# MLP of the second block: the first block of the up projection as eight products of quarters, its weights loaded before the mixer's last matmuls, sums of x made beside it

## The chip, the cores and the metric

One core of a Trainium2 chip runs the whole program. The metric is the device time of one execution in microseconds (us). The engines are named as in the profile: PE (TensorE matmuls), PEld (its weight loads), DVE (VectorE), ACT (ScalarE), POOL (GpSimd), SP (SyncE, whose queue issues the DMAs).

## The reference, cut to what matters

The model is two blocks: two layers of attention, mLSTM and SSD with a mixture of experts, then one hybrid layer (gated delta rule and RG-LRU) with an MLP, over 512 tokens of width 1024 in float32. The change concerns the MLP at the end of the second block alone (`d_ff` is 4096, taken in 8 blocks of 512 columns by the kernel):

```python
x = x + jnp.einsum("bse,ed->bsd", mix, w_out.astype(dt))
m = rmsnorm(x, norm_mlp_w)
u = jax.nn.relu(jnp.einsum("bsd,df->bsf", m, w_ff1.astype(dt)))
x = x + jnp.einsum("bsf,fd->bsd", u * u, w_ff2.astype(dt))
...
return rmsnorm(x, final_norm_w)
```

## The kernel before, in words

**Split numbers.** Every float32 operand of a large matmul is kept as two float32r tiles, a high and a low part (`HL`). `split` (L128 to L139) makes them: a cast on ACT writes the high part (L134), a subtraction on DVE or POOL writes the low part (L139). `mm` (L122 to L126) then issues three matmuls: high by high, low by high, high by low.

**The MLP's products.** For each of the 8 blocks of 512 columns, `up(b)` computes relu(m @ w1)^2 with seven products instead of eight. The weights of a block are four quarters (two halves of the 1024 input rows by two halves of 256 columns), x is four quarters too (two halves of the input rows by two halves of 256 tokens): B11, B21, B12, B22. The seven products take sums of weight quarters and sums of x quarters (T1 to T4), and sums of the products are the four quarters of the result. One product is 24 matmuls of 128x256 (two halves of columns, four row tiles, three split matmuls each). `up_part(b, n, u)` makes the weights of product n: with n = 0 it loads two raw tiles of 1 MB (L254), with n = 2 it makes three sums on DVE (L260, L261, L262), with n = 5 a fourth (L264), and it splits the operand, the low part on POOL for n of 1 and 6 and on DVE otherwise. `down(b)` multiplies by w2: 96 matmuls of 128x512 into four PSUM banks `dn`, each emptied on DVE by an addition to R (L1837). The order is up(0), up(1), down(0), up(2), down(1), and so on to down(7).

**The mixer before it, and the joint.** The MLP's input is R plus the second half of the mixer's output projection (`out_last`, additions to R at L1866), which runs by token tiles i = 0 to 3 of 128 tokens. After each tile `fin(i)` takes the rms norm (sum of squares on ACT, L1326; the root on DVE, L158 to L166; the scaling on DVE, L1333, which reads the gain from the tile `sw`) and `mlp_in` transposes the result (PE, L1770) into PSUM banks `tr`, copies it to the float32 tiles X32 (ACT, L1771) and makes the x operands. In the profile X32 is named uTh and uTl, whose space it takes. For tiles 0 and 1 these are B11 and B21; for tiles 2 and 3 `mlp_in` also makes the four sums of x (L1779, L1780, L1783, L1786) and splits T1 to T4 and B22. Two weight operands of block 0 (`w0`, named T3 and T4, whose space they take) are made before the mixer's last matmuls, and `fin(2)` issues the first two products of block 0 with them (named dn<-B11,T3 and dn<-B21,T4 in the profile). The other five operands of block 0 are tasks in the plan, made when their ring slots are free.

**What sets the order.** Weight tiles stand in a list (`plan`); `pump` takes the next one when its ring of split tiles has a free slot, and the raw tiles come from two pools of two buffers each (raw0 and, after the mixer, raw1). Instructions of the functions here are put in order on each engine's queue by the framework's scheduler, so the order of the queues differs from that of the code. Sums of weights use the tile `sw` (`q[4]` at n = 2), which also holds the norm's gain until the last L1333 has read it.

Of the kernel before, what the change touches and what calls it, by code (L numbers as in the profile page):

```python
# [26 lines left out]
UNIT = 1024  # L27
# [43 lines left out]
class Kernel:  # L71
# [169 lines left out]
    def by_k(u):  # L241
        u = u.rearrange("p (k n) -> p k n", k=4)
        return [u[:, k] for k in range(4)]

    def up_part(self, b, n, u):

        v = self.nc.vector
        if n == 0:
            self.quarters = []
            for j in range(2):  # L250
                raw = self.t(self.raws[self.nraw % len(self.raws)].pool, "raw", [P, 2 * UNIT])
                self.nraw += 1
                at = b * 512 + j * 256
                self.nc.sync.dma_start(raw.rearrange("p (k n) -> p k n", n=256),  # L254
                                       self.a["w_ff1_2"][0][:, at:at + 256].rearrange("(k p) n -> p k n", p=P))
                self.quarters += [raw[:, 0:UNIT], raw[:, UNIT:2 * UNIT]]
        q = self.quarters
        if n == 2:
            q.append(self.t(self.mlpp, "sw", [P, UNIT]))
            v.tensor_tensor(q[4], q[2], q[3], op=OP.add)  # L260
            v.tensor_tensor(q[2], q[0], q[2], op=OP.subtract)  # L261
            v.tensor_tensor(q[0], q[4], q[0], op=OP.subtract)  # L262
        if n == 5:
            v.tensor_tensor(q[1], q[1], q[0], op=OP.subtract)  # L264
        self.split(u, q[(0, 1, 0, 4, 2, 1, 3)[n]], "act", "pool" if n in (1, 6) else "dve")
# [1490 lines left out]
        x.close()  # L1756
        return mix[0]

    def mlp_in(self, m, i, n, X, X32):


        nc, v = self.nc, self.nc.vector
        tk, half = slice(i % 2 * P, i % 2 * P + P), i // 2
        cut = lambda n: HL(X[n].h[:, :, tk], X[n].l[:, :, tk])
        ps = []
        for g in range(2):
            p = self.ps("tr", [P, 4, P])
            for j in range(4):
                f = 4 * g + j
                nc.tensor.transpose(p[:, j, :], n[:, f * P:(f + 1) * P], self.ident)  # L1770
            nc.scalar.copy(X32[g][:, :, i * P:(i + 1) * P], p)  # L1771
            if not half:
                self.split(cut(("B11", "B21")[g]), p)
            ps.append(p)
        if not half:
            return
        (b11, b12), (b21, b22) = [[x[:, :, z + i % 2 * P:z + i % 2 * P + P] for z in (0, 256)] for x in X32]
        t2 = self.t(m, "u2", [P, S], bufs=2).rearrange("p (k t) -> p k t", k=4)
        v.tensor_tensor(b11, b12, b11, op=OP.subtract)  # L1779
        v.tensor_tensor(t2, b22, b11, op=OP.subtract)  # L1780
        self.split(cut("T2"), t2)
        self.split(cut("T1"), b11)
        v.tensor_tensor(b12, b22, b12, op=OP.subtract)  # L1783
        self.split(cut("T3"), b12)
        self.split(cut("B22"), ps[1])
        v.tensor_tensor(b21, b21, t2, op=OP.subtract)  # L1786
        self.split(cut("T4"), b21)

    def up_product(self, p, w, x):
        for z in range(2):  # L1790
            for k in range(4):
                self.mm(p[:, z * 256:(z + 1) * 256], w[k][:, z * P:(z + 1) * P], x[:, k, :], start=k == 0, stop=k == 3)

    def mlp(self, m, X, R, begun, finish):

        nc, v = self.nc, self.nc.vector
        uT = {}

        def up(b):
            u_ = self.hl(m, "uT", [P, 4, S], bufs=2)  # L1800
            s1, s5, s3, _ = [t[:, z:z + S] for t in [self.t(m, "nrm", [P, D], bufs=2) for _ in range(2)] for z in (0, S)]

            def keep(f, t, x, y):

                u = self.t(m, "u2", [P, S], bufs=2)
                v.tensor_tensor(u, x, y, op=OP.add)  # L1806
                v.scalar_tensor_tensor(u, u, 0.0, u, op0=OP.max, op1=OP.mult)  # L1807
                d = HL(*(x[:, 2 * f:2 * f + 2, 256 * t:256 * t + 256] for x in (u_.h, u_.l)))
                self.split(d, u.rearrange("p (f t) -> p f t", f=2), "act")

            def product(n, x):
                p = self.ps(("mm", "tr")[n % 2], [P, S])
                self.up_product(p, self.take(("up", b, n)), X[x])
                self.done(("up", b, n))
                return p

            A, C = (product(0, "B11"), product(1, "B21")) if b else begun
            nc.scalar.copy(s1, A)
# [21 lines left out]
            for hf in range(2):  # L1840
                self.done(("dn", b, hf))

        up(0)
        for b in range(8):
            if b < 7:
                up(b + 1)
            if b == 6:
# [3 lines left out]
                finish = lambda i: fin(i, g2)  # L1851
            down(b)

    def second(self):
        nc, a, v = self.nc, self.a, self.nc.vector
        with ExitStack() as c:
            rp = self.pool(c, "res2")
            R = self.t(rp, "R", [P, NT, D])
# [11 lines left out]
            rp = self.pool(c, "mlp")  # L1870
            self.mlpp = rp
            g = self.t(rp, "sw", [P, D])
            self.bcast_load(g, a["norm_mlp_w_2"][0], D)
            X, begun = {}, []

            w0 = [self.hl(rp, t, [P, UNIT]) for t in ("T3", "T4")]
            for n in range(2):
                self.up_part(0, n, w0[n])
            for t in ("B11", "B21", "B22", "T1", "T2"):
                X[t] = self.hl(rp, t, [P, 4, 256])  # L1880
            X32 = self.hl(rp, "uT", [P, 4, S], bufs=2)
            X32 = [x.bitcast(F32) for x in (X32.h, X32.l)]

            def fin(i):
                n = self.t(rp, "nrm", [P, D], bufs=2)
                if i == 2:
                    for z in range(2):
                        p = self.ps("dn", [P, S])
                        self.up_product(p, self.by_k(w0[z]), X[("B11", "B21")[z]])
                        begun.append(p)  # L1890
                    for t in ("T3", "T4"):
                        X[t] = self.hl(rp, t, [P, 4, 256])
                self.rms(rp, n, R[:, i], g, jk=n)
                self.mlp_in(rp, i, n, X, X32)
                self.dump("x3", R[:, i], i)

            self.out_last(mixT, [("out2", q) for q in (2, 3)], add, [4, 5, 6, 7, 0, 1, 2, 3], fin)
# [1 line left out]
            with ExitStack() as x1:  # L1899
# [8 lines left out]
                        nc.sync.dma_start(self.out[0, i * P:(i + 1) * P, :], o)  # L1908
                    self.dump("out", o, i)

                self.mlp(rp, X, R, begun, finish)

    def plan(self):

        a, T = self.a, []
        add = lambda *z, **k: T.append(Task(*z, **k))
        for l in range(2):
            w = a["w_in"][l]
# [24 lines left out]
        w = a["w_in_2"][0]  # L1943
# [10 lines left out]
        w2 = a["w_ff2_2"][0]  # L1954

        def up(b):
            for n in range(0 if b else 2, 7):
                add(("up", b, n), "p", [], 4, 256)
                T[-1].make = lambda u, n=n: self.up_part(b, n, u)

# [282 lines left out]
```

## Time and profile before

| what | value |
|---|---|
| median of 3 runs | 1737.26 us (1736.63 to 1739.16) |
| the profiled execution's own time | 1732.17 us |
| its span, first to last instruction | 1730.3 us |
| mean granted clock of TensorE | 0.954 |
| PE busy in the span | 1561.6 us (90%) |
| DVE busy | 1298.5 us (75%) |
| ACT busy | 827.2 us (48%) |
| POOL busy | 561.3 us (32%) |

The own time is 1.87 us over the span: what lies before the first and after the last instruction. The shares are averages over stages with different limits. The MLP begins at about 1360 us of the span and ends with it. A table of windows tells for stretches of the span how busy each engine was and which clock TensorE was granted; the waits tell what ended an engine's idle time; the timeline gives single instructions with their start and duration. A matmul's duration includes the time in the array's pipeline: its rate is read from the distance between starts.

### The profile page before, as it was taken

Reading aid. Unit: us, or ns where it says so; the run is one execution under the profiler, and the core shown is the slowest. Engines: PE = TensorE matmul, PEld = TensorE weight load, DVE = VectorE, ACT = ScalarE, POOL = GpSimd, SP = SyncE. Lnnn points to the kernel's source line nnn. Section 1 sums busy time; section 2 is a strip of 40 time slices with the busy share of each in tenths; the row PEclk is TensorE's granted clock in tenths of the full one; section 3 lists DMA queues with packets and bytes.
Section 4 is the critical chain, followed back from the end, with each engine's and each line's share of the span. In section 5 each row is a group of like instructions: output and inputs, shape, how many; then the busy total and the mean of one; then the engine's idle time right before and its main releaser. Section 6 shows DMA issues by size and latency. Waiting matters only on the chain. (4 is left out here: it accounts for less than half of the span.)

```text
span 1730.3 us, 29609 instructions
## 1 busy us (share of the span) xinstructions
PE 1561.6 (90%) x11539; PEld 1398.0 (81%) x11539; DVE 1298.5 (75%) x2480; ACT 827.2 (48%) x1422; POOL 561.3 (32%) x464
## 2 busy tenths in 40 slices
PE   7899999699956899997889993999799799999997
PEld 6789899698946789887878972887578698899996
DVE  6847963789957847865689977777776797777774
ACT  4354562278856344551368863555532533333331
POOL 0555332316114555334315202003411143444341
PEclk9999999899987999999989996999999899999999
DMA  5214123499945211123399964432112243333311
GB/s 183 61 59 147 64 103 115 180 363 357 396 166 204 61 59 48 50 86 131 127 346 358 373 239 170 128 98 74 38 52 75 73 127 117 98 98 98 98 62 49
DMA packets 107662, 248.02 MB, mean 143 GB/s; under 512 B 9460, under 2 KB 70776, under 8 KB 95224
## 3 DMA queue, kind: packets, MB, share of 16 engines
q1 hardware_dynamic: 101624, 225.05, 37.4%
q0 software_dynamic: 5888, 20.97, 3.8%
q8 instruction: 94, 1.54, 0.4%
q14 instruction: 56, 0.46, 0.1%
HBM read 218.21 MB, written 27.79 MB: 142 GB/s over the span
## 5 line engine op out<-in xcount | busy, mean ns | idle before, releaser
L134 ACT CAST wh<-raw 128x1024 fp32r<-128x1024 f32 (+3 forms) x375 | 377.5, 1024 | 278.4 <-PE mm L126 70.3
L139 POOL TENSOR_TENSOR wl<-raw,wh 128x1024 fp32r<-128x1024 f32 (+3 forms) x117 | 281.3, 2414 | 474.7 <-ACT wh L134 469.0
L139 DVE TENSOR_TENSOR wl<-raw,wh 128x1024 fp32r<-128x1024 f32 (+2 forms) x258 | 307.2, 1211 | 64.3 <-ACT wh L134 63.4
L124 PE MATMUL mm<-wh,actTh 128*128 128x256 f32 (+2 forms) x640 | 189.5, 297 | 22.2 <-ACT wh L134 7.9
L126 PE MATMUL mm<-wh,actTl 128*128 128x256 f32 (+2 forms) x640 | 185.7, 292 | 2.9 <-POOL actTl L139 2.4
L125 PE MATMUL mm<-wl,actTh 128*128 128x256 f32 (+2 forms) x640 | 185.9, 291 | 0.5 <-DVE wl L139 0.5
L124 PE MATMUL mm<-actTh,wh 128*128 128x512 f32 x368 | 150.5, 409 | 2.4 <-DVE FD L509 0.8
L126 PE MATMUL mm<-actTh,wl 128*128 128x512 f32 x368 | 148.0, 402 | 0.0
L125 PE MATMUL mm<-actTl,wh 128*128 128x512 f32 x368 | 148.0, 402 | 0.0
L124 PEld LDWEIGHTS mm<-wh,actTh 128*128 128x128 f32 x640 | 124.9, 195 | 25.2 <-ACT wh L134 7.9
L126 PEld LDWEIGHTS mm<-wh,actTl 128*128 128x128 f32 x640 | 123.9, 194 | 5.4 <-POOL actTl L139 3.3
L125 PEld LDWEIGHTS mm<-wl,actTh 128*128 128x128 f32 x640 | 124.8, 195 | 1.8 <-DVE wl L139 0.9
L1089 POOL DMA_INDIRECT G<-Xd,idx x32 | 77.9, 2434 | 131.1 <-DVE oh L1138 58.3
L124 PE MATMUL dn<-wh,uTh 128*128 128x512 f32 x256 | 100.9, 395 | 3.1 <-DVE R L1837 3.1
L126 PE MATMUL dn<-wh,uTl 128*128 128x512 f32 x256 | 100.4, 392 | 0.0
L125 PE MATMUL dn<-wl,uTh 128*128 128x512 f32 x256 | 100.1, 391 | 0.1
L124 PEld LDWEIGHTS mm<-actTh,wh 128*128 128x128 f32 x368 | 70.6, 192 | 17.8 <-PE mm L126 2.2
L126 PEld LDWEIGHTS mm<-actTh,wl 128*128 128x128 f32 x368 | 70.9, 193 | 14.4
L125 PEld LDWEIGHTS mm<-actTl,wh 128*128 128x128 f32 x368 | 71.0, 193 | 14.0
L124 PE MATMUL py<-wh,GTh 128*96 128x256 f32 x256 | 73.6, 287 | 1.3 <-ACT wh L134 1.3
L124 PE MATMUL pg<-wh,GTh 128*96 128x256 f32 x256 | 74.3, 290 | 0.0
L125 PE MATMUL py<-wl,GTh 128*96 128x256 f32 x256 | 72.9, 285 | 1.1 <-DVE wl L139 1.1
(781 smaller groups left out, 4308.4 us busy)
## 6 DMA issues: line engine op xcount, KB each, us to landing
raw<-in_expert_w_gate_dram SPq DMA_DIRECT2D x32, 1024.0 KB, 10.4
raw<-in_expert_w_up_dram SPq DMA_DIRECT2D x32, 1024.0 KB, 10.3
raw<-in_expert_w_down_dram SPq DMA_DIRECT2D x32, 1024.0 KB, 10.9
raw<-in_w_ff_dram SPq DMA_DIRECT2D x32, 1024.0 KB, 5.5
raw<-in_w_in_dram SPq DMA_DIRECT2D x27, 1024.0 KB, 5.4
raw<-in_w_out_dram SPq DMA_DIRECT2D x12, 1024.0 KB, 5.2
Yd<-Ye SPq DMA_DIRECT2D x32, 384.0 KB, 6.7
Yd<-zr SPq DMA_DIRECT2D x9, 512.0 KB, 6.4
```

Of the source, the lines that this page charges most:

```text
L124: mm(out, lhsT.h, rhs.h, start=start, stop=False, **kw)
L125: mm(out, lhsT.h, rhs.l, start=False, stop=False, **kw)
L126: mm(out, lhsT.l, rhs.h, start=False, stop=stop, **kw)
L134: nc.scalar.copy(dst.h, src)
L139: (nc.gpsimd if leng == "pool" else nc.vector).tensor_tensor(dst.l, src, dst.h, op=OP.subtract)
L1089: nc.gpsimd.indirect_dma_start(out=G[:n], out_offset=None, in_=self.Xd, in_offset=bass.IndirectOffsetOnAxis(ap=idx[:n], axis=0))
```

## The change

The first block of the up projection, which took seven products of sums, is computed as the plain eight products of quarters (`up_plain`), each pair summed in PSUM. Its four weight quarters are loaded and split by `up_block0` before the mixer's last matmuls, two low parts on DVE and two on POOL, into tiles named T2, T1, T3 and T4; the tasks of block 0 leave the plan, so that none of its weight sums is made. `mlp_in` makes the four x quarters alone, for every token tile; B12 stands in one of the two raw0 buffers (named raw in the profile). The four sums of x, and the splits of T1 to T4, are made once for all 256 columns in `mlp_sums` beside the products of block 0, and are first needed by up(1). The results of block 0 are emptied by an ACT relu and one DVE multiplication per quarter.

```diff
+    def up_load(self, b):
+        q = []
+        for j in range(2):
+            raw = self.t(self.raws[self.nraw % len(self.raws)].pool, "raw", [P, 2 * UNIT])
...
+    def up_block0(self, ws):
+        for n, (q, w) in enumerate(zip(self.up_load(0), ws)):
+            self.split(w, q, "act", ("dve", "pool")[n // 2])
...
-    def mlp_in(self, m, i, n, X, X32):
+    def mlp_in(self, i, n, X, X32):
...
+            x = X[f"B{g + 1}{half + 1}"]
+            self.split(HL(x.h[:, :, tk], x.l[:, :, tk]), p)
             nc.scalar.copy(X32[g][:, :, i * P:(i + 1) * P], p)
-            if not half:
-                self.split(cut(("B11", "B21")[g]), p)
-            ps.append(p)
-        if not half:
-            return
-        (b11, b12), (b21, b22) = [[x[:, :, z + i % 2 * P:z + i % 2 * P + P] for z in (0, 256)] for x in X32]
-        t2 = self.t(m, "u2", [P, S], bufs=2).rearrange("p (k t) -> p k t", k=4)
+
+    def mlp_sums(self, X, X32):
+        v = self.nc.vector
+        (b11, b12), (b21, b22) = [[x[:, :, z:z + 256] for z in (0, 256)] for x in X32]
         v.tensor_tensor(b11, b12, b11, op=OP.subtract)
-        v.tensor_tensor(t2, b22, b11, op=OP.subtract)
-        self.split(cut("T2"), t2)
-        self.split(cut("T1"), b11)
         v.tensor_tensor(b12, b22, b12, op=OP.subtract)
-        self.split(cut("T3"), b12)
-        self.split(cut("B22"), ps[1])
-        v.tensor_tensor(b21, b21, t2, op=OP.subtract)
-        self.split(cut("T4"), b21)
+        v.tensor_tensor(b22, b22, b11, op=OP.subtract)
+        v.tensor_tensor(b21, b21, b22, op=OP.subtract)
+        return dict(T1=b11, T2=b22, T3=b12, T4=b21)
...
+        def up_plain():
+            u_ = self.hl(m, "uT", [P, 4, S], bufs=2)
+            W = [self.by_k(w) for w in w0]
+            C, T = [], {}
+            for f, t in ((0, 0), (1, 0), (0, 1), (1, 1)):
+                p = self.ps("dn", [P, S])
+                for z in range(2):
+                    for k in range(KD):
+                        x = X[f"B{k // 4 + 1}{t + 1}"][:, k % 4]
+                        self.mm(p[:, z * 256:(z + 1) * 256], W[2 * f + k // 4][k % 4][:, z * P:(z + 1) * P], x,
+                                start=k == 0, stop=k == KD - 1)
+                C.append((f, t, p))
+                if (f, t) == (0, 0):
+                    T = self.mlp_sums(X, X32)
+                for n in {(0, 1): ("T2", "T1"), (1, 1): ("T3", "T4")}.get((f, t), ()):
+                    X[n] = self.hl(m, n, [P, 4, 256])
+                    self.split(X[n], T[n])
+            for f, t, p in C:
+                r, u = self.t(m, "nrm", [P, D], bufs=2)[:, 0:S], self.t(m, "u2", [P, S], bufs=2)
+                nc.scalar.activation(r, p, AF.Relu)
+                v.tensor_tensor(u, r, r, op=OP.mult)
+                self.split(HL(*(x[:, 2 * f:2 * f + 2, 256 * t:256 * t + 256] for x in (u_.h, u_.l))),
+                           u.rearrange("p (f t) -> p f t", f=2), "act")
+            uT[0] = u_
...
-            A, C = (product(0, "B11"), product(1, "B21")) if b else begun
+            A, C = product(0, "B11"), product(1, "B21")
...
-        up(0)
+        up_plain()
...
-            w0 = [self.hl(rp, t, [P, UNIT]) for t in ("T3", "T4")]
-            for n in range(2):
-                self.up_part(0, n, w0[n])
-            for t in ("B11", "B21", "B22", "T1", "T2"):
-                X[t] = self.hl(rp, t, [P, 4, 256])
+            w0 = [self.hl(rp, t, [P, UNIT]) for t in ("T2", "T1", "T3", "T4")]
+            self.up_block0(w0)
+            X = {t: self.hl(rp, t, [P, 4, 256]) for t in ("B11", "B21", "B22")}
+            b12 = self.t(self.raw0.pool, "raw", [P, 2 * UNIT]).bitcast(FR).rearrange("p (z k t) -> p z k t", z=2, k=4)
+            X["B12"] = HL(b12[:, 0], b12[:, 1])
...
-                if i == 2:
-                    for z in range(2):
-                        p = self.ps("dn", [P, S])
-                        self.up_product(p, self.by_k(w0[z]), X[("B11", "B21")[z]])
-                        begun.append(p)
-                    for t in ("T3", "T4"):
-                        X[t] = self.hl(rp, t, [P, 4, 256])
...
         def up(b):
-            for n in range(0 if b else 2, 7):
+            for n in range(7 if b else 0):
```

Beside the weight operands made before the mixer's last matmuls (two casts more on ACT, one low part more on DVE and one more on POOL) and some exchanged neighbours among the norms, the queues are as before up to the end of the mixer. The first place is DVE, right behind the scaling of token tile 3 (L1333). The names are: wl the low part of a weight operand, sw and raw the weight sums (and raw<-tr the low part of B12), uTh and uTl the tiles X32 of x and, later, the block's result, u its square, nrm the relu. Before:

```order
L1333 SCALAR_TENSOR_TENSOR nrm<-R,rmrs,sw 128x1024
L139 TENSOR_TENSOR wl<-raw,wh 128x1024
L260 TENSOR_TENSOR sw<-raw 128x1024
L1779 TENSOR_TENSOR uTh<-uTh 128x4x128
L139 TENSOR_TENSOR B22l<-tr,B22h 128x4x128
L261 TENSOR_TENSOR raw<-raw 128x1024
L1779 TENSOR_TENSOR uTh<-uTh 128x4x128
L1780 TENSOR_TENSOR u_16623<-uTl,uTh 128x512
L1783 TENSOR_TENSOR uTh<-uTl,uTh 128x4x128
L139 TENSOR_TENSOR T1l<-uTh,T1h 128x4x128
```

With the change:

```order
L1342 SCALAR_TENSOR_TENSOR nrm<-R,rmrs,sw 128x1024
L139 TENSOR_TENSOR wl<-raw,wh 128x1024
L139 TENSOR_TENSOR raw<-tr,raw 128x4x128
L269 TENSOR_TENSOR sw<-raw 128x1024
L139 TENSOR_TENSOR B22l<-tr,B22h 128x4x128
L1822 TENSOR_TENSOR u_16921<-nrm 128x512
L270 TENSOR_TENSOR raw<-raw 128x1024
L139 TENSOR_TENSOR uTl<-u_16921,uTh 128x2x256
L271 TENSOR_TENSOR raw<-sw,raw 128x1024
L139 TENSOR_TENSOR raw<-tr,raw 128x4x128
```

The weight sums at this place were those of block 0 and are now those of block 1, and the sums of x have moved back behind the emptying of block 0's first quarter; counted from the first wl of these pieces up to the addition that frees the bank of up(1)'s last product (L1820 before, L1848 with the change), the queue with the change holds 19 instructions of 128x1024 and 15 of 128x512.

The second place is PE, right behind the last matmul of block 0 that needs token tiles 0 and 1 alone. Before:

```order
L126 MATMUL dn<-B21h,T4l 128x256
L1770 MATMUL tr<-ident,nrm 128x128 x13
L124 MATMUL tr<-T1h,wh 128x256
L125 MATMUL tr<-T1l,wh 128x256
L124 MATMUL mm<-T2h,wh 128x256
L124 MATMUL mm<-T3h,wh 128x256
L124 MATMUL tr<-B22h,wh 128x256
```

With the change (raw is B12, T2 and T3 hold weights of block 0, mm<-B11 is the first product of up(1)):

```order
L126 MATMUL dn<-B21h,T4l 128x256
L124 MATMUL mm<-B11h,wh 128x256
L1776 MATMUL tr<-ident,nrm 128x128 x4
L125 MATMUL mm<-B11l,wh 128x256
...
L124 MATMUL dn<-raw,T2h 128x256
L124 MATMUL dn<-raw,T3h 128x256
```

What followed the transposes were products of block 0 that need weight sums; now it is the first product of up(1), whose weights are a plain quarter, and then the products of block 0 for tokens 256 to 511. The third place is SP's queue, from the load of the norm's gain on. Before:

```order
L150 DMA sw<-in_norm_mlp_w_dram 128x1024
L254 DMA raw<-in_w_ff_2_dram 128x8x256 x4
L229 DMA raw<-in_w_ff_2_dram 128x4x512 x2
L254 DMA raw<-in_w_ff_2_dram 128x8x256 x2
L229 DMA raw<-in_w_ff_2_dram 128x4x512 x2
```

With the change:

```order
L150 DMA sw<-in_norm_mlp_w_dram 128x1024
L252 DMA raw<-in_w_ff_2_dram 128x8x256 x4
L229 DMA raw<-in_w_ff_2_dram 128x4x512
L252 DMA raw<-in_w_ff_2_dram 128x8x256 x2
L229 DMA raw<-in_w_ff_2_dram 128x4x512 x3
```

The second load of down(0)'s weights (128x4x512) stood before the two loads of up(2) and now stands behind them. On PE, 7 of down(0)'s 96 matmuls now stand ahead of up(1)'s last two products, and 89 behind them.

## Rows read from the trace of the kernel before

**Rows 1.** Windows: us, busy of PE, PEld, DVE, ACT, POOL, PEclk, DMA, GB/s.
```profile
1340.00:1360.40 20.40, 20.40 (x177) 20.28 (x175) 13.90 (x37) 9.32 (x16) 2.49 (x1) 1.00 0.21 69
1366.60:1379.40 12.80, 1.92 (x14) 1.21 (x12) 10.90 (x15) 8.92 (x15) 0.00 (x0) 0.72 0.16 51
1379.40:1389.40 10.00, 7.25 (x26) 6.04 (x27) 10.00 (x13) 4.03 (x6) 0.00 (x0) 0.50 0.22 59
1389.40:1420.60 31.20, 31.20 (x264) 31.20 (x263) 30.78 (x31) 14.36 (x18) 14.78 (x5) 1.00 0.39 119
1432.00:1435.20 3.20, 0.06 (x2) 0.01 (x1) 3.20 (x4) 0.62 (x1) 0.85 (x1) 1.00 0.00 0
...
1446.40:1720.80 274.40, 274.40 (x1681) 245.75 (x1679) 199.21 (x221) 91.25 (x107) 107.32 (x39) 1.00 0.28 91
```

**Rows 2.** Waits of PE, 1360 to 1446: us in total, times, longest us.
```profile
PE tr L124 <- ACT wh L134: 9.1, 2, 7.9
PE dn L124 <- DVE R L1837: 3.1, 1, 3.1
PE tr L1770 <- ACT uTh L1771: 3.0, 2, 1.7
PE tr L126 <- DVE wl L139: 1.0, 1, 1.0
```

**Rows 3.** Timeline of PE: start us, us, engine, line, operation, tiles, idle before.
```profile
1360.37 0.28 PE L124 MATMUL dn<-B11h,T3h 128*128 128x256 f32 x1
...
1363.30 0.28 PE L124 MATMUL dn<-B21h,T4h 128*128 128x256 f32 x1
...
1435.19 0.51 PE L124 MATMUL dn<-wh,uTh 128*128 128x512 f32 x1 [3.14 <-DVE R L1837]
...
1446.24 0.28 PE L124 MATMUL mm<-B11h,wh 128*128 128x256 f32 x1
```

**Rows 4.** Timeline of ACT (first row) and DVE.
```profile
1367.37 1.04 ACT L134 CAST wh<-raw 128x1024 fp32r<-128x1024 f32 x1 [4.73 <-DMA raw<-in_w_ff_dram]
...
1368.50 1.23 DVE L139 TENSOR_TENSOR wl<-raw,wh 128x1024 fp32r<-128x1024 f32 x1 [2.50 <-ACT wh L134]
...
1378.46 0.69 DVE L1786 TENSOR_TENSOR uTl<-uTl,u 128x512 f32<-128x512 f32 x1
1379.06 0.68 DVE L139 TENSOR_TENSOR T1l<-uTh,T1h 128x512 fp32r<-128x512 f32 x1
...
1382.60 1.22 DVE L139 TENSOR_TENSOR wl<-raw,wh 128x1024 fp32r<-128x1024 f32 x1
1383.74 1.22 DVE L139 TENSOR_TENSOR wl<-sw,wh 128x1024 fp32r<-128x1024 f32 x1
```

**Rows 5.** Groups by shape, 1389 to 1434, DVE; then POOL's timeline and group.
```profile
L139 DVE TENSOR_TENSOR uTl<-u,uTh 128x512 fp32r<-128x512 f32 x7 | 7.9, 1132 | 0.1
L1807 DVE SCALAR_TENSOR_TENSOR u<-u 128x512 f32<-128x512 f32 x8 | 7.6, 945 | 0.1
L262 DVE TENSOR_TENSOR raw<-sw,raw 128x1024 f32<-128x1024 f32 x2 | 6.3, 3134 | 0.0
...
L261 DVE TENSOR_TENSOR raw<-raw 128x1024 f32<-128x1024 f32 x2 | 4.5, 2237 | 0.1
L1806 DVE TENSOR_TENSOR u<-nrm 128x512 f32<-128x512 f32 x2 | 2.8, 1396 | 0.1
...
1405.31 2.40 POOL L139 TENSOR_TENSOR wl<-raw,wh 128x1024 fp32r<-128x1024 f32 x1 [9.31 <-ACT wh L134]
...
L139 POOL TENSOR_TENSOR wl<-raw,wh 128x1024 fp32r<-128x1024 f32 x7 | 22.2, 3181 | 46.5 <-ACT wh L134 46.5
```

**Rows 6.** SP's timeline; landing of L229's loads; the page's DMA issues.
```profile
1360.56 0.99 SPq L254 DMA_DIRECT2D raw<-in_w_ff_dram  x2
...
DMA to landing us min/median/max: 4.9/5.1/5.5
...
raw<-in_expert_w_gate_dram SPq DMA_DIRECT2D x32, 1024.0 KB, 10.4
```

More of the change, by code (lines that the diff above doesn't have):

```diff
@@ L243, in by_k @@
         return [u[:, k] for k in range(4)]
+    def up_load(self, b):
+        q = []
+        for j in range(2):
+            raw = self.t(self.raws[self.nraw % len(self.raws)].pool, "raw", [P, 2 * UNIT])
+            self.nraw += 1
+            at = b * 512 + j * 256
+            self.nc.sync.dma_start(raw.rearrange("p (k n) -> p k n", n=256),
+                                   self.a["w_ff1_2"][0][:, at:at + 256].rearrange("(k p) n -> p k n", p=P))
+            q += [raw[:, 0:UNIT], raw[:, UNIT:2 * UNIT]]
+        return q
+    def up_block0(self, ws):
+        for n, (q, w) in enumerate(zip(self.up_load(0), ws)):
+            self.split(w, q, "act", ("dve", "pool")[n // 2])
     def up_part(self, b, n, u):
@@ L248, in up_part @@
         if n == 0:
[L249 to L256, printed above, removed]
+            self.quarters = self.up_load(b)
         q = self.quarters
@@ L1757, in hybrid @@
         return mix[0]
-    def mlp_in(self, m, i, n, X, X32):
-        nc, v = self.nc, self.nc.vector
+    def mlp_in(self, i, n, X, X32):
+        nc = self.nc
         tk, half = slice(i % 2 * P, i % 2 * P + P), i // 2
-        cut = lambda n: HL(X[n].h[:, :, tk], X[n].l[:, :, tk])
-        ps = []
         for g in range(2):
@@ L1792, in up_product, with mlp @@
                 self.mm(p[:, z * 256:(z + 1) * 256], w[k][:, z * P:(z + 1) * P], x[:, k, :], start=k == 0, stop=k == 3)
-    def mlp(self, m, X, R, begun, finish):
+    def mlp(self, m, X, X32, w0, R, finish):
         nc, v = self.nc, self.nc.vector
         uT = {}
+        def up_plain():
[22 more added lines that the diff above has]
+            uT[0] = u_
         def up(b):
@@ L1873, in second @@
             self.bcast_load(g, a["norm_mlp_w_2"][0], D)
-            X, begun = {}, []
-            w0 = [self.hl(rp, t, [P, UNIT]) for t in ("T3", "T4")]
-            for n in range(2):
-                self.up_part(0, n, w0[n])
-            for t in ("B11", "B21", "B22", "T1", "T2"):
-                X[t] = self.hl(rp, t, [P, 4, 256])
+            w0 = [self.hl(rp, t, [P, UNIT]) for t in ("T2", "T1", "T3", "T4")]
[3 more added lines that the diff above has]
+            X["B12"] = HL(b12[:, 0], b12[:, 1])
             X32 = self.hl(rp, "uT", [P, 4, S], bufs=2)
@@ L1885, in fin @@
                 n = self.t(rp, "nrm", [P, D], bufs=2)
-                if i == 2:
-                    for z in range(2):
-                        p = self.ps("dn", [P, S])
-                        self.up_product(p, self.by_k(w0[z]), X[("B11", "B21")[z]])
-                        begun.append(p)
-                    for t in ("T3", "T4"):
-                        X[t] = self.hl(rp, t, [P, 4, 256])
                 self.rms(rp, n, R[:, i], g, jk=n)
-                self.mlp_in(rp, i, n, X, X32)
+                self.mlp_in(i, n, X, X32)
                 self.dump("x3", R[:, i], i)
@@ L1909, in finish @@
                     self.dump("out", o, i)
-                self.mlp(rp, X, R, begun, finish)
+                self.mlp(rp, X, X32, w0, R, finish)
     def plan(self):
```

## The prediction

> **What bounds the kernel now.** I read the windows first, from the end. From 1446.40 to 1720.80 PE is busy in all of 274.40 us at the full clock [rows 1]: there nothing but PE's work counts, the change does not touch it, and whatever moves its beginning moves the end by as much. So the question is when up(2) begins, which is the row at 1446.24 [rows 3]. The mixer's last matmul ends before 1360.37, where the first product of block 0 starts, and up to there PE is just as full: 20.40 of 20.40 [rows 1]. What lies between, 85.9 us, is the place of the change.
>
> There PE works 1.92 us of 12.80 and then 7.25 of 10.00 at a granted clock of 0.72 and 0.50, so 1.2 GHz in the second stretch, behind the long wait in the first, while DVE is busy in 10.90 and 10.00 [rows 1]. In the next 31.20 us PE is full again, but DVE too, with 30.78 [rows 1]: it runs behind, and that comes out at 1432, where PE waits 3.14 us for DVE's addition to R to free a bank [rows 1, 3]. The waits name the rest: 9.1 us for casts of weights (for block 0 most are made from DVE's weight sums), 3.0 us for copies of x, 1.0 us for a low part [rows 2]. Together 16.2 us. The half clock adds half of 7.25 and 0.28 of 1.92, 4.1 us. So PE loses about 20.3 us here, and the engine behind it is DVE.
>
> **The change part by part.** *PE.* A product is 24 matmuls: from 1360.37 to 1363.30, 2.93 us [rows 3]. Block 0 had seven and has eight: 2.93 us more. A matmul of down is (1446.24 - 1435.19) / 48 = 0.230 us [rows 3].
>
> *Weights of block 0.* Of DVE's queue behind the mixer go four sums and four low parts of 128x1024, at 1.14 us from start to start [rows 4], 9.1 us. Into the stretch before the mixer's end come one such low part on DVE, two casts on ACT and one low part on POOL of 2.40 us [rows 5]. There DVE is busy 13.90 us, ACT 9.32 and POOL 2.49 of 20.40, under a full PE [rows 1]; I cost them at nothing. If that cover failed, they would cost at most 1.14 and 2.40 us, once.
>
> *Emptying block 0.* Seven additions, four squares and four low parts of 128x512 become four squares and four low parts: seven times 0.60 us [rows 4] less, 4.2 us. Relus on ACT replace two copies; ACT is not the bound, with 14.36 of 31.20 [rows 1].
>
> *x.* Sums and splits are the same elements in longer instructions; B12 is split in addition, two times 0.60 us. Net, DVE has 9.1 + 4.2 - 1.2 = 12.1 us less to do behind the mixer.
>
> *When the path is free.* PE has the eight products of block 0, for which no weight sum is needed, and up(1)'s first two, so it should wait for next to nothing until the later products of up(1). Of these the last needs the bank that L1848 frees. So I count DVE's queue. It starts as before with the first low part of up(1)'s weights, at 1368.50: the load is issued at 1360.56 behind the same matmul and is there at 1367.37 [rows 4, 6]. Up to and with L1848 stand 19 instructions of 1.14 and 15 of 0.60 us, 30.7 us: 1399.2 with nothing in the way.
>
> What is in the way is POOL. DVE's instructions with both inputs in SBUF grow while POOL splits: uTl 1132 ns where it takes 686 without, L1807 945, L262 3134 and L261 2237 where 1221 is usual, L1806 from nrm 1396 [rows 5], against the usual durations of [rows 4]. The excess is 3.1 + 2.1 + 3.8 + 2.0 + 1.4 = 12.4 us for 7 splits, 1.78 us each. With the change, six low parts of POOL fall into the counted stretch (two of up(1), four of down(0)'s weights), and the last may come behind it. Five cost 8.9 us, six 10.7; I take the middle, 9.8: L1848 ends at 1409.0. Below it is nothing (1399.2, and then PE is the bound), above it six full splits of 2.40 us, 14.4: 1413.6. I take the mean excess, since it was measured on the same instructions.
>
> The Trainium skill has a rule here, in SBUF — State Buffer, "Who interferes with whom": an instruction of VectorE with two inputs in SBUF and one of GpSimd that reads SBUF shut each other out, and the one that is first keeps the shared ports for its whole length. By it the excess of 12.4 us is a lock, which the rows agree with, and a weight split more on POOL is no free relief; at 2.40 us for each of six splits the sum would be 4.6 us worse than mine.
>
> *The sum.* Last product from 1409.0, 2.93 us; then 89 matmuls of down(0) that stand behind it, 89 x 0.230 = 20.5. up(2) begins at 1432.4 instead of 1446.24: **13.8 us less**. This supposes that down(0) no longer waits for DVE. The first addition to R stands 11 instructions behind L1848, nine of 0.60 and two of 1.14, 7.7 us, and one hold of 1.78: 1418.5. PE wants that bank after 41 more matmuls, at 1411.9 + 9.4 = 1421.3. The cover is 2.8 us; without it up to the old 3.14 us comes back.
>
> *Clock.* PE's new waits are spread over the last two products of up(1). The old wait of 3.14 us left the clock at 1.00 [rows 1], so I cost them nothing more.
>
> Against the profiled execution this makes a span of 1716.5 us and an own time of 1718.4 (1732.17 before). The median of the runs is 5.1 us above that execution, and I carry the difference over: 1737.26 - 13.8 = 1723.5.
>
> **The rivals.** *PE is the bound at once.* If DVE keeps ahead, all of the 20.3 us go, less 2.93: 17.4 us, 1719.9. For it: most waits of PE are for sums that are no longer made [rows 2]. Against: DVE has no slack in 1389 to 1420 [rows 1]. Chance 0.10.
>
> *Full holds.* Every split of POOL holds DVE for its length: L1848 at 1413.6, a gain of 9.2, 1728.1. For it: L262 grew by 1.9 us in the mean. Against: the others grew by 0.3 to 1.0 [rows 5]. 0.13.
>
> *A third transfer.* The first load of down(0) now goes out right behind up(1)'s two. Loads of 1 MB that stand in longer rows take 10.4 us in the expert layers against 6.8 here [rows 4, 6]. If the first landing slips by these 3.6 us, DVE's whole queue does: a gain of 10.2, 1727.1. Against: it is issued last of the three. 0.10.
>
> *The clock falls.* A new wait of PE of several us near 1400 leaves a stretch at 1.2 GHz, as the wait of 7.9 us did [rows 1, 2], at the same price of 4.1 us: a gain of 9.7, 1727.6. Against: 3.14 us did nothing. 0.08. The Trainium skill (TensorE: Matmul & The Clock Gate, "HAM oscillation — how this bites in real kernels") warns of kernels that fall back to the low clock at every gap between bursts; by it the waits that I leave would cost this again.
>
> *Slower: down(0)'s second load.* B12 keeps one raw0 buffer until PE has read it, and that load now stands in SP's queue behind both loads of up(2), which wait for the last reader of up(1)'s raw tiles. By the same count (10 of 1.14, 7 of 0.60, two holds) that reader is done at about 1388. The load needs 5.1 us, a cast of 1.04 and a low part of 2.40 [rows 4, 5, 6], 8.5 in all, and is wanted at 1413.1, so it must go out by 1404.6. It decides from there, microsecond for microsecond; slower than before needs 1418.4, 30 us later than counted. For it: the block is on SP's queue, where nothing passes. 0.04.
>
> *It doesn't do what it says.* If the quarters were not split by 1360.6, PE would wait at once. POOL is idle but for 2.49 of 20.40 us there [rows 1], and needs 4.8. A wait that eats the gain: 0.03.
>
> **How the numbers follow.** The forecast keeps 0.52. A measurement of this kernel tells about 0.2%, 3.5 us, from no change. All cases but the last two are faster by more: 0.93; same 0.03, slower 0.04. The range takes in PE as the bound (1719.9) and the single misfortunes down to 9 us of gain (1728.1), with half a us for the runs' spread on each side: 1719 to 1729. Two of them together and the last two cases stay out.
>
> **What would show it.** In the profile after: no wait of PE for casts of weights between 1366 and 1385, and no half clock there; the first product of up(1) inside block 0; DVE without a gap from about 1368 to 1410, at L1848 near 1409; waits of PE of some 3 to 5 us in all before up(1)'s last product; the next up's first matmul at 1432 and PE full from there to the end. Wrong would be: a wait for a load of w2 at down(0); DVE's first low part of up(1) later than 1369; a granted clock under 1 after 1360; or a start of up(2) outside 1428 to 1437.

## The result, and the profile after

The change makes the kernel faster: 1719.0 us (median of 4 runs, 1717.57 to 1722.29) against 1737.93 (4 runs on the same chip), a ratio of 0.9894, 95% interval 0.9876 to 0.9912. A second, longer comparison (e1, below) gives 0.9914, 0.9894 to 0.9934. The profiled execution took 1717.64 us with a span of 1715.7, so 14.6 us less span than before.

PE's timeline, against [rows 3], shows where block 0 begins and where up(2) does:

```profile
1360.18 0.28 PE L124 MATMUL dn<-B11h,T2h 128*128 128x256 f32 x1
...
1431.37 0.28 PE L124 MATMUL mm<-B11h,wh 128*128 128x256 f32 x1
```

The stretch between these two rows, called **the stretch** from here on, takes 71.19 us and took 85.87: 14.68 less, all that the span lost. It is also free of what differs from execution to execution before the MLP: over all profiles here block 0 begins between 1359.89 and 1365.92 us. So I compare kernels by the stretch.

The windows, with the columns of [rows 1]:

```profile
1340.00:1360.40 20.40, 20.03 (x172) 19.80 (x171) 14.94 (x38) 11.62 (x18) 5.74 (x2) 1.00 0.15 50
1366.60:1379.40 12.80, 12.40 (x105) 12.18 (x104) 10.93 (x12) 10.26 (x16) 2.51 (x1) 1.00 0.36 127
1379.40:1389.40 10.00, 10.00 (x86) 10.00 (x85) 9.96 (x9) 4.21 (x6) 2.42 (x1) 1.00 0.46 126
1389.40:1420.60 31.20, 28.37 (x189) 25.56 (x189) 30.90 (x29) 13.09 (x17) 17.65 (x5) 1.00 0.39 129
1433.00:1706.00 273.00, 272.93 (x1668) 244.03 (x1666) 198.86 (x219) 90.23 (x106) 105.02 (x39) 1.00 0.28 91
```

Where PE worked 1.92 us of 12.80 and then 7.25 of 10.00 at half clock, it works 12.40 and 10.00 at the full clock. DVE is as busy as it was, 10.93 and 9.96. PE's waits in the stretch, against [rows 2]:

```profile
PE dn L125 <- POOL wl L139: 1.7, 1, 1.7
PE dn L124 <- DVE R L1865: 1.2, 1, 1.2
PE tr L1776 <- ACT uTl L1779: 0.4, 1, 0.4
```

The balance over the stretch: PE's time without work falls from 85.87 - 69.04 = 16.83 to 71.19 - 67.95 = 3.24 us, 13.6 less; its busy time falls by 1.1, which is 2.9 for the extra product less, by difference, 4.0 for the half clock that is gone. Together 14.7.

DVE's queue from its first split of up(1) to its first addition to R, with one row of POOL (fifth):

```profile
1367.81 1.23 DVE L139 TENSOR_TENSOR wl<-raw,wh 128x1024 fp32r<-128x1024 f32 x1 [2.34 <-ACT wh L134]
...
1370.39 2.02 DVE L269 TENSOR_TENSOR sw<-raw 128x1024 f32<-128x1024 f32 x1 [0.45 <-DMA raw<-in_w_ff_dram]
...
1379.87 0.68 DVE L139 TENSOR_TENSOR B22l<-tr,B22h 128x512 fp32r<-128x512 f32 x1
1380.47 3.23 DVE L139 TENSOR_TENSOR wl<-raw,wh 128x1024 fp32r<-128x1024 f32 x1
...
1395.65 6.44 POOL L139 TENSOR_TENSOR wl<-raw,wh 128x1024 fp32r<-128x1024 f32 x1 [13.03 <-ACT wh L134]
...
1399.78 0.68 DVE L1834 TENSOR_TENSOR u<-nrm,tr 128x512 f32<-128x512 f32 x1
1400.38 2.27 DVE L139 TENSOR_TENSOR uTl<-u,uTh 128x512 fp32r<-128x512 f32 x1
1402.57 2.89 DVE L1835 SCALAR_TENSOR_TENSOR u<-u 128x512 f32<-128x512 f32 x1
1405.38 0.67 DVE L1848 TENSOR_TENSOR nrm<-nrm,mm 128x512 f32<-128x512 f32 x1
...
1408.20 2.88 DVE L139 TENSOR_TENSOR uTl<-u,uTh 128x512 fp32r<-128x512 f32 x1
...
1414.72 2.92 DVE L1835 SCALAR_TENSOR_TENSOR u<-u 128x512 f32<-128x512 f32 x1
...
1419.30 0.67 DVE L1865 TENSOR_TENSOR R<-R,dn 128x512 f32<-128x512 f32 x1
```

An instruction that lasts 1.22 or 0.68 us undisturbed and stands here with 2 to 3.2 was held while POOL split. The excess up to L1848 is 0.8 + 2.0 + 1.6 + 2.2 = 6.6 us. Behind it, up to the addition to R, come 2.2 + 2.2 and 0.65 of an L1834 that is not shown: 5.1. Seven splits of POOL cost 11.7 us, 1.67 each.

The holding goes both ways. POOL's split of 1395.65, the first of down(0)'s weights, took 6.44 us where 2.40 is usual [rows 5]. DVE had five instructions in a row with all operands in SBUF, the first already running, and the split ended at 1402.09, 2.3 us behind the start of L1834, the next with an operand in PSUM (tr). This low part is the one that PE waited 1.66 us for, until 1402.15.

The chain that ended last (start, us, what) runs through this queue, from up(1)'s load to that addition:

```profile
1360.79 9.47 DMA raw<-in_w_ff_dram
1370.39 2.02 DVE sw L269
...
1419.37 0.61 DVE R L1865
```

### The profile page after: what moved, and what is told of

It is laid out like the page before. It is cut to its first block, busy times and chain, and to the rows that moved or that the text cites. A ratio compares the mean times of both kernels' runs of the same rounds, so it can differ in the third digit from the quotient of the medians.

```text
span 1715.7 us, 29630 instructions
## 1 busy us (share of the span) xinstructions
PE 1563.6 (91%) x11563; PEld 1399.2 (82%) x11563; DVE 1283.1 (75%) x2460; ACT 825.1 (48%) x1419; POOL 553.3 (32%) x464
## 5 line engine op out<-in xcount | busy, mean ns | idle before, releaser
L134 ACT CAST wh<-raw 128x1024 fp32r<-128x1024 f32 (+3 forms) x371 | 373.0, 1024 | 261.8 <-PE mm L126 71.9
L139 POOL TENSOR_TENSOR wl<-raw,wh 128x1024 fp32r<-128x1024 f32 (+3 forms) x116 | 276.6, 2394 | 459.7 <-ACT wh L134 454.0
L1098 POOL DMA_INDIRECT G<-Xd,idx x32 | 72.1, 2252 | 134.7 <-DVE oh L1147 58.6
L125 PE MATMUL pg<-wl,GTh 128*96 128x256 f32 x256 | 73.8, 288 | 0.0
```

The costliest lines, as they stand in the source:

```text
L125: mm(out, lhsT.h, rhs.l, start=False, stop=False, **kw)
L134: nc.scalar.copy(dst.h, src)
L139: (nc.gpsimd if leng == "pool" else nc.vector).tensor_tensor(dst.l, src, dst.h, op=OP.subtract)
L1098: nc.gpsimd.indirect_dma_start(out=G[:n], out_offset=None, in_=self.Xd, in_offset=bass.IndirectOffsetOnAxis(ap=idx[:n], axis=0))
```

## The experiments

All stretches, each from one profile, with PE's time without work in them (stretch less PE's busy time of the windows):

| kernel | stretch, us | PE idle, us |
|---|---|---|
| before | 85.87 | 16.83 |
| changed | 71.19 | 3.24 |
| e1 changed, again | 70.84 | 2.93 |
| e2 POOL's six splits on DVE | 66.92 | 0.00 |
| e3 squares on ACT | 73.57 | 4.28 |
| e4 a ninth product | 71.94 | 1.66 |
| e5 four more sums on DVE | 74.59 | 4.97 |
| e6 both e2 and e5 | 70.91 | 1.96 |
| e7 before, POOL's splits on DVE | 80.88 | 12.57 |
| e8 half the weights late | 76.16 | 6.51 |
| e9 before, no sums in block 0 | 85.90 | 14.89 |
| e10 x sums by tile | 80.82 | 10.72 |
| e11 POOL's two of up(1) on DVE | 67.82 | 0.65 |
| e12 both e2 and e3 | 68.59 | 1.44 |

The two profiles of the changed kernel differ by 0.35 us. The runs are coarser: on the chip of e1 (median 1721.39 us) e2 took 1715.74, e3 1721.80 and e4 1720.17, so they tell e2 from the changed kernel, but not e3 and e4; e5, e6 and e8 to e11 ran once. The last column leaves out what a fallen clock costs: PE's busy time, 67.95 us in the changed kernel, is 69.29 in e3, 69.62 in e5, 69.65 in e8 and 70.10 in e10, for the same matmuls.

**e1.** No edit.

> The changed kernel itself, once more, in more rounds. The stretch from block 0's first product to the first matmul of up(2) took 85.87 us before and 71.19 in the first profile of the change, 14.7 less, while the medians of the runs lay 18.9 apart. Theory (all of the gain lies in that stretch): the ratio of the runs comes out near 1 - 14.7/1737 = 0.9915, between 0.990 and 0.993, and the stretch again takes 71.2 us within 0.5. Rival (the change also gives something elsewhere, or the first comparison was no fluke): 0.9894 or less again.

1721.39 us against 1737.8, ratio 0.9914; the stretch took 70.84. The gain is the stretch's, and the 18.9 us between the first medians were partly spread.

**e2: POOL's six splits on DVE.**

```diff
-        self.split(u, ..., "act", "pool" if n in (1, 6) else "dve")
+        self.split(u, ..., "act", "pool" if n in (1, 6) and b > 1 else "dve")
...
-                self.set_phase("p", ..., [("act", "pool")])
+                self.set_phase("p", ..., [("act", "dve")] * 4 + [("act", "pool")] * 28)
```

> The changed kernel with six of POOL's low parts (the two of up(1), the four of down(0)) given to DVE. Theory (DVE is held whenever POOL splits, so those six cost DVE nearly what DVE would pay to do them): DVE gets 6 x 1.14 = 6.8 us more and loses about 9.4 us of holds, so the stretch is 0 to 2.8 us shorter than 71.2, PE's wait of 1.7 us for POOL's low part is gone, and DVE's instructions there last 1.2 and 0.68 us throughout. Rival (POOL's splits run free beside DVE): up(1)'s last products come up to 6.8 us later and the stretch takes 75 to 78 us.

66.92 us, and 1715.74 us (0.988 of before, 0.986 to 0.990) where e1 took 1721.39 on the same chip: better than both kernels. PE is full in every window:

```profile
1365.00:1385.00 20.00, 20.00 (x169) 19.88 (x168) 17.28 (x28) 12.80 (x20) 0.00 (x0) 1.00 0.49 158
1385.00:1405.00 20.00, 20.00 (x169) 19.96 (x169) 20.00 (x20) 11.00 (x16) 0.00 (x0) 1.00 0.49 159
1405.00:1432.00 27.00, 27.00 (x141) 23.04 (x140) 23.14 (x31) 8.94 (x11) 2.43 (x1) 1.00 0.25 78
```

Two of DVE's groups by shape, 1376 to 1420, in the changed kernel and then in e2 (busy us, mean ns, idle before):

```profile
L139 DVE TENSOR_TENSOR uTl<-u,uTh 128x512 fp32r<-128x512 f32 x6 | 7.9, 1314 | 0.1
...
L1835 DVE SCALAR_TENSOR_TENSOR u<-u 128x512 f32<-128x512 f32 x3 | 6.5, 2162 | 0.0
```

```profile
L139 DVE TENSOR_TENSOR uTl<-u,uTh 128x512 fp32r<-128x512 f32 x6 | 4.1, 686 | 0.0
...
L1835 DVE SCALAR_TENSOR_TENSOR u<-u 128x512 f32<-128x512 f32 x3 | 2.1, 685 | 0.0
```

With POOL silent neither group of DVE is stretched. The holds were POOL's, and a split costs DVE less when it makes it itself. The gain, 4.1 us against the mean of the two changed profiles, is above the 2.8 that I expected at most, since PE's waits went altogether.

**e3: squares on ACT.**

```diff
-                v.tensor_tensor(u, r, r, op=OP.mult)
+                nc.scalar.activation(u, r, AF.Square)
```

> The changed kernel with the four squares of block 0's emptying on ACT in place of DVE, 4 x 0.60 = 2.4 us less for DVE. Theory (PE is nearly the bound, DVE sets only the 1.2 us wait for the first addition to R): the stretch gets 1 us shorter, 0 to 1.5. Rival (DVE's queue decides, microsecond for microsecond): 2.4 us shorter. Second rival (ACT's longer queue makes the casts of down(0)'s weights late): the wait for POOL's low part grows and the stretch gets up to 2 us longer.

None of the three: 2.6 us longer in the profile. The order on DVE moved a little, and POOL's splits fell on other instructions (DVE twice, then POOL):

```profile
1387.89 3.33 DVE L1787 TENSOR_TENSOR uTl<-uTl,uTh 128x1024 f32<-128x1024 f32 x1
...
1399.83 3.44 DVE L139 TENSOR_TENSOR T4l<-uTl,T4h 128x1024 fp32r<-128x1024 f32 x1
...
1383.78 6.36 POOL L139 TENSOR_TENSOR wl<-raw,wh 128x1024 fp32r<-128x1024 f32 x1 [10.23 <-ACT wh L134]
```

POOL's split of 2.4 us lasted 6.36, and DVE's excess up to L1848 came to 0.6 + 2.1 + 2.2 + 1.6 + 2.2 = 8.7 us against 6.6, with another 1.0 of waiting for a load: more than the 2.4 saved. PE waited 1.0 us for L1834 and 2.6 us for L1848, which the changed kernel just avoids. Behind these the granted clock fell to 0.50 (1412 to 1414), and 1.4 of the 2.6 us are PE's busy time.

**e4: a ninth product.**

```diff
+                if (f, t) == (1, 1):
+                    for k in range(KD):
+                        x = X[f"B{k // 4 + 1}{t + 1}"][:, k % 4]
+                        self.mm(p[:, 256:512], W[2 * f + k // 4][k % 4][:, P:2 * P], x, start=k == 0, stop=k == KD - 1)
```

> The changed kernel with one more product's worth of matmuls in block 0: 24 of those of its last output are made twice, 2.93 us of PE's work that changes nothing. Theory (PE is the bound but for 2.8 us of waits for DVE and POOL behind 1400): the stretch gets longer by 1.5 to 2.9 us. Rival (DVE's queue decides, and PE's work is hidden in waits): the waits of 1.7 and 1.2 us go, and the stretch gets longer by 0.1 to 0.5 us.

0.9 us longer than the mean of the changed profiles (71.0), between the two: of 2.93 us of work two thirds disappear in waits. PE's only wait over a quarter us is now the one for DVE's addition to R:

```profile
1423.18 0.50 PE L124 MATMUL dn<-wh,uTh 128*128 128x512 f32 x1 [1.65 <-DVE R L1869]
```

It ends 60.8 us into the stretch, against 59.9 (1420.03) in the changed kernel. So DVE's chain still sets the end there; it follows PE's delay by only 1.0 us.

**e5: four more sums on DVE.**

```diff
-            v.tensor_tensor(q[4], q[2], q[3], op=OP.add)
+            for _ in range(5 if b == 1 else 1):
+                v.tensor_tensor(q[4], q[2], q[3], op=OP.add)
```

> The changed kernel with the first weight sum of up(1) made five times over, so DVE has 4 x 1.14 = 4.6 us more to do ahead of up(1)'s later products (as before the change, when block 0's sums stood there). Theory (DVE's queue, holds by POOL included, reaches L1848 only 0.3 us before PE wants the bank): the stretch from block 0's first product to up(2) gets 3.5 to 5 us longer than 71.0 (71.2 and 70.8 in the two profiles). Rival (PE is the bound and DVE has time to spare): 0 to 1 us longer.

3.6 us longer, as much as the theory gave, but PE did not wait for L1848. It waited for T2's low part, then 0.75 us for one of a weight, and at the end for the addition to R:

```profile
1395.63 0.38 PE L125 MATMUL mm<-T2l,wh 128*128 128x256 f32 x1 [1.25 <-DVE T2l L139]
...
1425.94 0.50 PE L124 MATMUL dn<-wh,uTh 128*128 128x512 f32 x1 [2.60 <-DVE R L1866]
```

Behind the first two waits the granted clock fell to 0.50 (1398 to 1400), and 1.7 of the 3.6 us are PE's busy time. Nor is the rest DVE's work alone: a split of POOL begun at 1393.41 lasted 11.34 us, so that up(2)'s loads, which need its raw tile, went out at 1404.78, 42.1 us into the stretch instead of 22.5, and DVE stood 3.06 us for one of them. So DVE has no 4.6 us to spare here; what its work alone would cost is not shown.

**e6: e2 and e5 together.**

> The same four extra sums, but in the kernel whose six low parts of POOL are on DVE (its stretch: 66.9 us, PE never waits). Theory (without POOL's holds DVE has slack: its L1848 ended 5.8 us before the last product of up(1) began): 0 to 1.5 us longer. Rival (DVE's queue is as tight there as in the changed kernel): 3.5 to 5 us longer.

4.0 us longer than e2: the rival's amount. I had taken the slack from L1848, but the tight place is earlier, the split of T2. Its wait is short, and a second one follows; then the clock falls. PE's timeline, and the windows behind it:

```profile
1396.68 0.38 PE L125 MATMUL mm<-T2l,wh 128*128 128x256 f32 x1 [1.26 <-DVE T2l L139]
1397.77 0.50 PE L124 MATMUL dn<-wh,uTh 128*128 128x512 f32 x1 [0.70 <-ACT wh L134]
```

```profile
1396.00:1398.00 2.00, 0.62 (x2) 0.42 (x3) 2.00 (x3) 2.00 (x4) 0.00 (x0) 1.00 0.09 32
1398.00:1400.00 2.00, 2.00 (x12) 1.96 (x12) 2.00 (x3) 1.66 (x3) 0.00 (x0) 0.60 0.01 4
1400.00:1402.00 2.00, 2.00 (x12) 2.00 (x12) 2.00 (x3) 0.00 (x0) 0.00 (x0) 0.54 0.38 63
```

1.96 us of waits and 2.0 us of busy time more than in e2 (68.95 against 66.92): the half clock doubles the price.

**e7: the kernel before, POOL's splits on DVE.** The edit of e2, but in the kernel before, so that seven splits move: the two edits have the same lines, with `(b > 1 or (b, n) == (0, 1))` in place of `b > 1`.

> The kernel before the change with its seven low parts of POOL behind the mixer on DVE. Theory (before, DVE's queue set the end, and POOL held it 12.4 us for those seven): DVE gains 12.4 and pays 7 x 1.14 = 8.0, so the stretch gets 2 to 5 us shorter than 85.9. Rival (the early waits for weights made from DVE's sums, with the half clock behind them, decide): within 1 us of 85.9. Were it as good as the changed kernel with the same edit (66.9), the change itself would be worth nothing.

5.0 us shorter, 1730.98 us (0.9976 of before, 0.9964 to 0.9988). The theory's amount, at its upper end. The wait for the addition to R is gone, those for weights stay:

```profile
PE tr L124 <- ACT wh L134: 8.6, 2, 7.4
PE tr L1770 <- ACT uTh L1771: 2.5, 2, 1.3
```

From e7 to e2 the change without POOL is worth 80.88 - 66.92 = 14.0 us, nearly what it is worth with it: POOL's splits cost both kernels about the same (5.0 and 4.1 us), and the gain does not come from them.

**e8: half the weights late.** Quarters 2 and 3 of block 0 are loaded and split behind the mixer.

```diff
+        self.late[0]()
...
+                if i == 3:
+                    self.late[1](n)
```

`late[1](n)` copies one element of the last tile's normalised x into the raw tile, so that the load behind it waits, then loads and splits.

> The changed kernel, but the second half of block 0's weights (quarters 2 and 3) is loaded and split only behind the mixer: its load is held until the last token tile's normalised x is there, at about 5 us into block 0. Theory (PE is nearly the bound, so a wait early in block 0 is not made up): waits of PE for these weights of 4 to 9 us in all, a granted clock below 1 behind a long one, and a stretch 5 to 9 us longer than 71.0. Rival (DVE's queue decides, and early waits are made up by waits that go later): 0 to 2 us longer.

76.16 us, 5.2 longer, with waits spread over the first 25 us and a clock of 0.50 to 0.64 from 1374 to 1378, behind two waits of 1.24 and 1.29 us. The amount is the theory's, the waits are not: only one is for these weights,

```profile
PE dn L124 <- ACT T3h L134: 1.3, 1, 1.3
```

and the other early ones, 3.7 us, are for a copy of x, the low part of B22 and up(1)'s weights, of which the changed kernel has 0.4; whether the late load or the casts and low parts behind it delay them is not shown. PE still waits 1.5 us for the addition to R. So early waits are not made up, and the 5.2 us are the price of loading, casting and splitting half the weights late, 1.7 of them PE's busy time at the lower clock.

**e9: the kernel before without block 0's sums.**

```diff
+        if n == 2 and b == 0:
+            q.append(q[2])
-        if n == 2:
+        elif n == 2:
...
-        if n == 5:
+        if n == 5 and b:
```

> The kernel before the change with block 0's four weight sums left out: its products 2 to 6 use the loaded quarters as they are, so block 0 computes something else, with the same matmuls, casts and low parts. It does one part of the change alone. Theory (the waits for weights made from those sums, and the half clock behind them, are most of what the change took away): PE's wait of 9.1 us for casts shrinks to under 3 us, the clock stays at 1.00 or nearly, and the stretch is 8 to 13 us shorter than 85.9, that is 73 to 78. Rival (DVE's queue decides at its end): 4 x 1.14 = 4.6 us shorter, 81 to 82. Second rival (the casts then wait for something else on ACT or DVE at the same place): within 2 us of 85.9.

85.90, the second rival. The low parts, free to go at once, came on DVE's queue ahead of the last tile's norm, and PE stood before the transposes instead:

```profile
PE tr L1772 <- DVE nrm L1335: 9.9, 1, 9.9
```

At the end a single wait for the addition to R was followed by the half clock, which the 3.14 us in the kernel before were not [rows 1, 3]; PE's busy time is 2.0 us longer than there:

```profile
1434.36 0.80 PE L124 MATMUL dn<-wh,uTh 128*128 128x512 f32 x1 [2.72 <-DVE R L1839]
```

```profile
1436.00:1438.00 2.00, 2.00 (x7) 1.52 (x6) 1.84 (x4) 0.00 (x0) 0.00 (x0) 0.50 0.00 0
```

So e9 says nothing about the sums alone; their share of the gain stays open.

**e10: x sums by token tile.**

```diff
     def mlp_in(self, i, n, X, X32):
...
+        if half:
+            self.mlp_sums(X, X32, i % 2 * P, P)
```

> The changed kernel with the sums of x made by token tile again, as before the change, eight of 128x512 right behind the copies of tiles 2 and 3, in place of four of 128x1024 after block 0's first output. Theory (that part of the change is worth little: the same elements, 8 x 0.60 against 4 x 1.14 us): the stretch is within 1.5 us of 71.0. Rival (the sums stand ahead of the low parts of B22 and of up(1)'s first weights, and DVE has no slack at about 30 us into the stretch): 2 to 5 us longer, with a wait of PE there.

9.8 us longer, twice the rival's upper end and on another way. PE's one great wait is 8.8 us for DVE's L1838 (L1834 in the changed kernel), at 1414.10. Rows of DVE, POOL and SP:

```profile
1386.20 0.68 DVE L1789 TENSOR_TENSOR uTh<-uTh 128x512 f32<-128x512 f32 x1
...
1398.96 0.69 DVE L1826 TENSOR_TENSOR u<-nrm 128x512 f32<-128x512 f32 x1
1411.08 1.22 DVE L269 TENSOR_TENSOR sw<-raw 128x1024 f32<-128x1024 f32 x1 [11.43 <-DMA raw<-in_w_ff_dram]
...
1386.40 15.54 POOL L139 TENSOR_TENSOR wl<-raw,wh 128x1024 fp32r<-128x1024 f32 x1 [10.02 <-ACT wh L134]
...
1401.96 0.99 SPq L252 DMA_DIRECT2D raw<-in_w_ff_dram  x2
```

From 1386.20 to 1399.65 DVE had sixteen instructions in a row without a PSUM operand, and POOL's split, which arrived at 1386.40, ended 2.3 us behind the last of them: 15.54 us instead of 2.4. That split was the last reader of a raw tile of up(1); SP waited 16.8 us for it, and up(2)'s loads went out at 1401.96, 37.0 us into the stretch instead of 22.5 (1382.65 in the changed kernel). DVE, whose queue had the sum of up(2) next, stood 11.43 us, and with it all that PE needed. Of the 9.8 us 2.2 are PE's busy time, at a clock of 0.50 behind the wait.

**e11: only up(1)'s two splits on DVE.** The first line of e2's edit alone.

> The changed kernel with only the two low parts of up(1) taken from POOL to DVE; the four of down(0) stay on POOL. Theory (each split on POOL costs DVE a hold of about 1.6 us on average, and the four of down(0) in a row stand where PE's waits are): little is gained, the stretch is 70 to 71.5 us, and the four splits still hold DVE up to L1848. Rival (the early holds, up(1)'s, were what made DVE late): 67 to 68.5, nearly all that moving six gave.

67.82, the rival: two splits give 3.2 of the 4.1 us. POOL's wait of 1.7 us is gone although the four splits of down(0) stay on POOL, beginning 32.2 us into the stretch instead of 35.5, because ACT made the cast before them earlier (1392.81, 31.1 us into the stretch, instead of 34.3). That start is not what freed PE: the first of them was kept longer,

```profile
1393.92 8.13 POOL L139 TENSOR_TENSOR wl<-raw,wh 128x1024 fp32r<-128x1024 f32 x1 [40.15 <-ACT wh L134]
```

and ended, as in the changed kernel, 2.3 us behind the start of DVE's L1834. L1834 began 38.0 us into the stretch instead of 39.6: DVE had two splits of 1.14 us more to do, but was free of 2.8 us of early holds, had begun 0.4 us earlier and waited 0.5 us less.

**e12: e2 and e3 together.**

> The four squares on ACT, which made the changed kernel's stretch 2.5 us longer, now in the kernel whose six low parts of POOL are on DVE. Theory (there the squares were not to blame but the holds by POOL, which fell on other instructions; without POOL PE alone is the bound): 66.5 to 67.5 us, no wait of PE over 0.5. Rival (ACT's longer queue makes casts late): 68 to 70, with waits for casts.

68.59, 1.7 longer than e2, with a wait of neither kind that I named: 1.44 us for B12's low part, which DVE made later in this order:

```profile
1383.89 0.39 PE L125 MATMUL dn<-raw,T2h 128*128 128x256 f32 x1 [1.44 <-DVE raw L139]
```

The squares are no relief even without POOL.

## Why the prediction was right

Forecast: up(2) at 1432.4, 13.8 us less, 1723.5 us. Measured: 1431.37, 14.7 us less, and 1719.0 and 1721.4 in the two comparisons, the first on the very edge of the range, the second well inside.

- *The end moves with up(2).* Right: PE works 272.93 of 273.00 us behind it.
- *PE loses 20.3 us in waits and half clock; the extra product costs 2.93.* Right: 16.83 and 4.0 by the balance; 3.24 us of waits are left, at a full clock.
- *Mixer-side splits at nothing.* Nearly: PE has 20.03 of 20.40 us, one wait of 0.4 for an addition to R.
- *L1848 ends at 1409.0, with 9.8 us of holds.* Mis-sized: 1406.05, with 6.6 (and a start 0.7 earlier). The price of a split was right (1.67 us in the mean, counted 1.78), its place was not: 5.1 us of the holds fall behind L1848, where I had counted one of 1.78.
- *The last product waits for L1848.* Wrong: it began at 1406.38 right behind the one before it, and PE's waits up to there were 2.1 us, not 3 to 5. PE came there no earlier, because it had waited 1.66 us for POOL's low part of down(0)'s weights, which I had costed at nothing. I had priced what POOL does to DVE and not what DVE does to POOL, although [rows 5] have POOL's seven splits at 3181 ns in the mean, against 2.40 us for one alone.
- *down(0) no longer waits for DVE.* Wrong by 1.17 us: I counted the first addition to R at 1418.5 against a want at 1421.3; it ended at 1419.97, and PE wanted the bank at 1418.86. My count stopped at the addition's start and left out its own 0.6 us; the larger part is holds, 5.1 us behind L1848 instead of 1.78. My clause for a failed cover named the place and an upper bound of 3.14.
- *New waits cost nothing in clock.* It came out so, 1.00 through the stretch, but the ground, one wait of 3.14 us that left the clock alone, was thin: in e9 a single wait of 2.72 us was followed by half clock.
- *The median lies 5.1 us above the profiled execution.* Mis-sized: it lies 1.4 above (1719.0 against 1717.64), and 0.2 in e1. The profiled execution of before was faster than all four runs that it is compared with here. This makes 3.7 of the 4.5 us between 1723.5 and 1719.0; the stretch makes the rest.

So the two waits that I left out stand where I had put the one that did not come. The last product began 2.6 us before my count and up(2) only 1.0: that the errors nearly cancel is luck. What the change takes away was right, and so was the engine: DVE's queue, with POOL's holds in it, sets the end still (an added 2.93 us on PE costs 0.9 in e4, an added 4.6 on DVE 3.6 in e5, half of it in clock).

Of the rivals, *PE is the bound at once* is what e2 makes true, with a stretch 19.0 us below before where I had counted 17.4. *Full holds* is refused by the mean of 1.67, though single holds reach 2.2. *A third transfer* did not show: DVE's first low part of up(1) began at 1367.81, before the 1368.50 of my count. Nor did *It doesn't do what it says*: PE had no wait at block 0's first product. *The clock falls* did not happen here, but it does in e3, e5, e6, e8, e9 and e10, behind waits from 0.7 to 8.8 us. *Slower through the loads* was not met either, with down(0)'s later loads issued from 1388.46 as counted (1388); e10 shows a near relative of it, up(2)'s loads held by the last reader of a raw tile, until 1402, and e5 another. The Trainium skill (SBUF — State Buffer, "Who interferes with whom") has the two engines shut each other out for whole instructions; single holds and e10 agree with it, while the mean over seven splits is 0.7 of a split's 2.4 us.

What the parts of the change are worth is not settled by one experiment each: half the weights loaded, cast and split late cost 5.2 us (e8), the x sums by token tile 9.8 (e10), by a wait for up(2)'s load that the kernel before did not have. What leaving out block 0's weight sums is worth alone stays open (e9).

## What to carry to other kernels

Read the gain from the place where the bounding engine stands idle, and count the whole queue behind it up to each point where that engine comes back for something: a sum of holds can be right and still fall behind another wait. A helper engine that holds up the one behind the bound is no relief there: taking two of POOL's splits back to DVE gave 3.2 us, taking six 4.1. In a queue this tight an edit that saves work can cost more by the order it brings (e3, e12), so look at who meets whom, not only at sums of durations; the two rest on one profile each.

## What was not expected of the hardware

- A split on POOL can be kept waiting by DVE for as long as DVE's instructions follow each other without a PSUM operand among them: 15.54 us in e10, 11.34 in e5, 8.13 in e11, 6.44 in the changed kernel and 6.36 in e3, against 2.4 alone. It came in when DVE reached an instruction with a PSUM operand (changed kernel, e11) or had a gap, 0.22 us in e5. In the changed kernel POOL's split at 1380.20 came in during one with a PSUM operand (1379.87, above) and held the next one, 3.23 us.
- The length of a wait of PE did not tell whether the clock falls. Pairs close together cost it: 1.26 and 0.70 us (e6) were followed by 0.60 and 0.54, 1.25 and 0.75 (e5) by 0.50, 1.24 and 1.29 (e8) by 0.50 to 0.64. Of single waits 3.14 us (before, [rows 1]) and 2.60 (e5) left it at 1.00, and 2.72 (e9) was followed by 0.50. 1.66 and 1.17 us, 16 us apart (changed kernel), left it at 1.00.
